# Due times for the last norm's operations, and for the conversions of the down weights in later rounds

## Chip, cores and metric

The kernel runs on one core of a Trainium2 chip. The metric is the time of one launch on the device in microseconds (us), as a median over runs; lower is better. All numbers are float32 at the interface. Matrix products run as three passes over a high and a low part of each operand, so that they keep float32 accuracy.

## The reference

An encoder of two layers on 1024 tokens of width 1024. Each layer mixes tokens (attention in layer 0, a pooling mixer in layer 1), attends to a memory, and applies a gated feed-forward network (FFN). A last RMS norm ends it. What bears on this change is the FFN's second product and that last norm:

```python
def rmsnorm(x, gain):
    y = x * lax.rsqrt(jnp.mean(x * x, axis=-1, keepdims=True) + EPS)
    return y * gain

def conv_gated_ffn(h, w_up, conv_w, conv_b, w_down):     # D_FF = 2816
    u = h @ w_up
    up = jnp.pad(u, ((0, 0), (1, 1), (0, 0)))
    u = up[:, :-2] * conv_w[0] + up[:, 1:-1] * conv_w[1] + up[:, 2:] * conv_w[2] + conv_b
    gate, val = u[..., :D_FF], u[..., D_FF:]
    return (jax.nn.silu(gate) * val) @ w_down

for i in range(2):
    ...                                                  # mixer, cross-attention
    x = x + conv_gated_ffn(rmsnorm(x, ffn_norm[i]), ...)
return rmsnorm(x, final_norm)
```

## The kernel before

**Rows.** The 1024 tokens lie in eight tiles of 128 rows, X0 to X7, each 1024 wide. "Row t" below is such a tile.

**The FFN's second product.** The gated values and `w_down` are multiplied by Strassen-like products: seven block products (numbers 1 to 7 in the table `PRODUCTS`) take the place of eight. The inner dimension is cut into units q of 256. The units are worked off in three rounds (`ROUNDS`, line 48): units 0 to 2, 3 to 6 and 7 to 9 in layer 0, and 0 to 2, 3 to 6 and 7 to 10 in layer 1. Within a round there are two groups g of four rows. Each group goes through the seven products in a fixed order, and each product is one accumulation on PE over the round's units, followed by one addition on DVE that reads the PSUM bank and adds it to half a row of X (line 1699). `plan_phase` (line 1708) writes all this down, and `plan_down` (line 1680) one product.

**Weights.** For each unit q, `plan_W` (line 1653) asks for four loads from HBM into scratch tiles (`scr`, six buffers for the whole kernel, line 658). They bring the operands B21 and B22 (one load), B11, T1 and T2 (one load), T3 and T4 (one load). Each of the seven operands is then converted: ACT copies it to its high part (line 664) and DVE subtracts that to get the low part (line 667), into a half slot of SBUF (40 halves in all). A scratch tile is free again when all its operands are converted. `plan_G` (line 1623) does the same for the gated values. The first product of a group in all but the last one uses B21, then follow B11, T1, T2, B22, T3 and T4.

**The order on the engines.** Nothing is issued in the order of the Python text. The class `Plan` (line 161) collects operations with an engine, a rough cost from the table `KINDS`, what they read and write, and the buffers that they take. PE's operations keep their order, and a clock runs along with PE's work. Every other operation gets a due time: with `late=`, it is PE's clock at that place of the text plus `late`; without it, it is infinite at first. `run` (line 228) then walks backwards and sets each due time to the smallest of (due time of a user of its result minus its own lag). So an operation without `late` is due just in time for PE, when PE uses its result in the end; when nobody does, its due time stays infinite. DVE, ACT, POOL and SP then take work by due time, the earliest first, as soon as inputs and buffers are there, and never more than 30 us of plan time ahead of it (`AHEAD`). An operation that takes a buffer is held back while operations with an earlier due time would lack one. The result is a fixed order of instructions for each engine; on the chip each engine works in that order and waits at each instruction for its inputs.

In these terms, before the change:

- The conversions of a round's units q have due times of 3, 6 or 9 us ahead of the round's first product, the same for all seven operands of a unit, but for the last unit of the round. That one has no `late`, so each operand is due for the product that uses it.
- The last norm's operations (`plan_final`, line 1752, in layer 1 alone) have no `late`, and no product reads their results. Their due time is infinite. For rows 0 to 6 they are: a sum of squares on ACT (line 726), two small POOL operations that make the reciprocal root (lines 718 and 720), one multiplication on DVE by root and gain (line 1747), and one store (line 1750). Row 7 is cut into parts: squares of the upper half and of a first quarter on ACT (line 1768), the gain on the upper half (line 1772, DVE), a sum (line 1776, DVE), the last quarter's squares and their sum (lines 1780 and 1782, DVE), the root (line 1786, POOL), then the upper half's scaling on ACT (line 1790) and the lower half's on DVE (line 1747), and two stores.

In the last round of layer 1 the second group runs its seven products first for rows 4 and 5 and then for rows 6 and 7, so rows 0 to 3 are complete at the end of the first group, and rows 4 and 5 in the middle of the second.

Of the kernel before, what the change touches and what calls it, by code (L numbers as in the profile page):

```python
# [628 lines left out]
class Kernel:  # L629
# [898 lines left out]
    def ffn_main(self, i, U, X, Xd, extra, out, begin):  # L1528
# [5 lines left out]
        C, fixed, half = {}, {}, U.half  # L1534
# [118 lines left out]
        def plan_W(plan, q, late):  # L1653
            def fetch(j):
                raws[q, j] = self.scr()
                if j < 2:
                    w = len(WAT[j]) * 512
                    nc.sync.dma_start(out=raws[q, j][:, :w], in_=wd[(2 * q + 1 - j) * P:(2 * q + 2 - j) * P, :w])
                else:
                    nc.sync.dma_start(out=raws[q, j].rearrange("p (n c) -> p n c", n=2),  # L1660
                                      in_=WT[q][2 * (j - 2):2 * (j - 1)].rearrange("n p c -> p n c"))

            def high(n, j, h):
                x = WD[q, n] = R.get_half()
                self.high(U.halves(x)[0], raws[q, j][:, h * 512:(h + 1) * 512])

            def low(n, j, h):
                self.low(*U.halves(WD[q, n]), raws[q, j][:, h * 512:(h + 1) * 512])
            for j, names in enumerate(WAT):
                raw = ("wraw", q, j)  # L1670
                plan.add("load", len(names) / 2, partial(fetch, j), (), [raw], [("scr", raw)])
                for h, n in enumerate(names):
                    k = ("w", q, n)
                    plan.add("copy", 512, partial(high, n, j, h), [raw], [k], [("half", k)], [raw])
                    plan.add("add", 512, partial(low, n, j, h), [raw, k], [k], uses=[raw, k], late=late)
                    plan.ended[k] = lambda n=n: R.put_half(WD.pop((q, n)))
# [31 lines left out]
        def plan_phase(plan, homes):  # L1708

            home = [X[t] for t in homes]  # L1710

            def plan_back(ts):
                for t in ts:
                    def back(t=t):
                        X[t] = home[t]
                        nc.sync.dma_start(out=X[t], in_=Xd[t * P:(t + 1) * P, :])
                    plan.add("load", 1, back, (), [(f"X{homes[t]}", j) for j in range(2)] + [("row", t, j) for j in range(2)])
            plan_back(range(NT - 2))
            if out is not None:
                plan_gain(plan)  # L1720
            for r, qs in enumerate(rounds):
                for k, q in enumerate(qs):
                    plan_W(plan, q, -3.0 * (len(qs) - 1 - k) if k < len(qs) - 1 else None)
                for g in range(2):
                    end = out is not None and (r, g) == (len(rounds) - 1, 1)
                    order = (1, 2, 6, 5, 7, 3, 4) if end else (2, 1, 5, 6, 3, 7, 4)
                    for js in ((0,), (1,)) if end else ((0, 1),):
                        for n in order:
                            plan_G(plan, r, qs, g, U.PRODUCTS[n][0], js)
                        for n in order:  # L1730
                            for j in js:
                                plan_down(plan, r, qs, g, js, j, n, *[(slice(0, 256), slice(256, 512))] * (end and (j, n) == (1, 4)))
                                yield
                                if (r, g, n, j) == (0, 0, 2, 0):
                                    plan_back(range(NT - 2, NT))


        last = {}

        def plan_gain(plan):  # L1740
            def fetch():
                last["gain"] = self.bcast(self.a["final_norm"])
            plan.add("load", 1, fetch, (), ["gain"], [("scr", "gain")], late=100.0)

        def scaled(t, r, c):
            x = X[t][:, c]
            nc.vector.scalar_tensor_tensor(x, x, r, last["gain"][:, c], op0=OP.mult, op1=OP.mult)

        def leave(t, c):
            nc.sync.dma_start(out=out[t * P:(t + 1) * P, c], in_=X[t][:, c])  # L1750

        def plan_final(plan, t, n, m):

            row, r, lo, hi = [("row", t, h) for h in range(2)], ("fr", t), slice(0, 512), slice(512, 1024)

            def junk(k):
                h = R.get_half()
                plan.ended[k] = lambda: R.put_half(h)
                return R.hv(h)

            def square():
                last[t] = self.row_rstd(X[t], junk(("fjunk", t)))

            def part(k, c):
                if t not in last:
                    last[t] = self.stat(4, "ss4")
                x = X[t][:, c]
                nc.scalar.activation(junk(("fjunk", t, k))[:, c], x, AF.Square, scale=D ** -0.5, accum_out=last[t][:, k:k + 1])

            def gained():  # L1770
                x = X[t][:, hi]
                nc.vector.tensor_tensor(out=x, in0=x, in1=last["gain"][:, hi], op=OP.mult)

            def sums():
                s = last[t]
                nc.vector.tensor_scalar(s[:, 0:1], s[:, 0:1], s[:, 1:2], EPS, op0=OP.add, op1=OP.add)

            def rest():
                s, x = last[t], X[t][:, 256:512]
                nc.vector.scalar_tensor_tensor(junk(("fjunk", t, 2))[:, 256:512], x, 1.0 / D, x, op0=OP.mult, op1=OP.mult,  # L1780
                                               accum_out=s[:, 2:3])
                nc.vector.tensor_tensor(out=s[:, 2:3], in0=s[:, 2:3], in1=s[:, 0:1], op=OP.add)

            def root():
                s = last[t]
                nc.gpsimd.tensor_tensor(out=s[:, 3:4], in0=s[:, 2:3], in1=self.mh[:, :1], op=OP.pow)

            def other():
                x = X[t][:, hi]
                nc.scalar.activation(x, x, AF.Copy, scale=last[t][:, 3:4])  # L1790

            def plan_part(kind, w, f, k, rows, writes):
                j = ("fjunk", t, k)
                plan.add(kind, w, f, rows, writes, [("half", j)], [j])

            if t < NT - 1 and n in (3, 4):
                j = ("fjunk", t)
                plan.add("square", 1024, square, row, [r], [("half", j)], [j])
                plan.add("tap", 1024, lambda: scaled(t, last[t], slice(0, 1024)), [r, "gain", *row], row, uses=["gain"])
                plan.add("load", 1, lambda: leave(t, slice(0, 1024)), row)  # L1800
            elif t == NT - 1 and n == 7:
                plan_part("square", 512, partial(part, 0, hi), 0, row[1:], [(r, 0)])
                plan.add("add", 512, gained, ["gain", *row[1:]], row[1:], uses=["gain"])
            elif t == NT - 1 and not m:
                plan_part("square", 256, partial(part, 1, slice(0, 256)), 1, row[:1], [(r, 1)])
                plan.add("tiny", 1, sums, [(r, 1)], [(r, 0)])
            elif t == NT - 1:
                plan_part("tap", 256, rest, 2, [(r, 0), *row[:1]], [(r, 2)])
                plan.add("scale", 1, root, [(r, 2)], [r])
                plan.add("copy", 512, other, [r, *row[1:]], row[1:])  # L1810
                plan.add("tap", 512, lambda: scaled(t, last[t][:, 3:4], lo), [r, "gain", *row[:1]], row[:1], uses=["gain"])
                for c, k in ((hi, row[1:]), (lo, row[:1])):
                    plan.add("load", 0.5, partial(leave, t, c), k)


        hl, raw = {}, {}
# [287 lines left out]
```

## Time and profile before

| what | value |
|---|---|
| median of 3 runs | 2538.62 us (2538.28 to 2541.3) |
| the profiled execution's own time | 2542.65 us |
| its span in the profile | 2540.9 us |
| granted TensorE clock | 0.996 |
| PE busy | 2486.5 us (98%) |
| DVE busy | 1998.7 us (79%) |
| ACT busy | 1350.8 us (53%) |
| POOL busy | 402.6 us (16%) |

The span is the time from the first to the last instruction in the profile, and it is 1.75 us shorter than the execution's own time. All instants below ("at 2519.24") are microseconds from the start of that span. "SPq" is the queue on which SyncE issues DMAs. A row of the timeline has the start, the busy time, the engine, the line, the operation, its tiles and a count; in brackets stands the idle time just before it and what ended it.

### The profile page before, as it was taken

How to read it: one execution, taken by the hardware profiler on the slowest of the kernel's cores; microseconds unless marked ns; L12 is line 12 of the kernel's file. 1: busy time of each engine (PE TensorE's matmuls, PEld its weight loads, DVE VectorE, ACT ScalarE, POOL GpSimd, SP SyncE). 2: the span in 40 equal slices, each digit the busy share in tenths (PEclk: the TensorE clock that was granted, in tenths of full speed). 3: DMA queues.
4: the chain of work that ended last, by engine and by line, in shares of the span. 5: the costliest groups of instructions: out<-in, count | busy, mean ns of one | idle time of the engine just before them, and what ended most of it. 6: DMA issues, size and time to landing. Idle time of an engine off the chain costs nothing.

```text
span 2540.9 us, 37074 instructions
## 1 busy us (share of the span) xinstructions
PE 2486.5 (98%) x13481; PEld 2132.1 (84%) x13481; DVE 1998.7 (79%) x2946; ACT 1350.8 (53%) x2301; POOL 402.6 (16%) x532
## 2 busy tenths in 40 slices
PE   8999999999999999999999999999999999999996
PEld 8998888888898888888877888889888888887785
DVE  7879999974986389888878766887469888878773
ACT  5558888862555255455455425545346455545441
POOL 5664554530001000000000003002000000000002
PEclk9999999999999999999999999999999999999998
DMA  4300000042595124333358654488124432447661
GB/s 157 94 18 1 2 1 1 1 158 71 172 320 185 62 72 124 93 115 104 94 174 273 205 161 118 138 279 297 60 67 116 117 111 83 118 138 259 221 197 70
DMA packets 306507, 320.71 MB, mean 126 GB/s; under 512 B 12821, under 2 KB 244349, under 8 KB 306325
## 3 DMA queue, kind: packets, MB, share of 16 engines
q1 hardware_dynamic: 306325, 318.35, 39.1%
q8 instruction: 106, 1.74, 0.3%
q14 instruction: 76, 0.62, 0.1%
HBM read 230.90 MB, written 82.58 MB: 123 GB/s over the span
## 4 chain that ended last, share of the span: by engine, by line
PE 82%; DVE 9%; ACT 3%; DMA 3%; issue 3%; POOL 1%; SPq 0%; DVEq 0%; POOLq 0%; ACTq 0%
PE pB L745 21%; PE pB L747 21%; PE pB L746 21%; PE pA L747 3%; PE pA L745 3%; PE pA L746 3%; PE pA L778 2%; DVE nm L788 2%; PE pB L739 2%; DVE R L667 2%; PE pB L1133 1%; DVE PT L673 1%; PE pB L1134 1%; ACT scr L791 1%; ACT R L664 1%
## 5 line engine op out<-in xcount | busy, mean ns | idle before, releaser
L745 PE MATMUL pB<-R,R 128*128 128x512 f32 (+1 forms) x2743 | 1020.5, 372 | 10.3 <-DVE X L1699 2.9
L746 PE MATMUL pB<-R,R 128*128 128x512 f32 (+1 forms) x2743 | 1013.2, 369 | 0.0
L747 PE MATMUL pB<-R,R 128*128 128x512 f32 (+1 forms) x2733 | 1009.8, 369 | 3.3 <-DVE R L667 3.2
L745 PEld LDWEIGHTS pB<-R,R 128*128 128x128 f32 x2743 | 517.6, 189 | 104.2 <-DVE X L1699 3.7
L747 PEld LDWEIGHTS pB<-R,R 128*128 128x128 f32 x2733 | 515.7, 189 | 91.2 <-DVE R L667 5.0
L746 PEld LDWEIGHTS pB<-R,R 128*128 128x128 f32 x2743 | 517.8, 189 | 85.7 <-DVE R L673 0.3
L664 ACT ACTIVATE R<-scr 128x512 fp32r<-128x512 f32 (+2 forms) x340 | 254.3, 780 | 245.5 <-PE pB L746 77.4
L667 DVE TENSOR_TENSOR R<-scr,R 128x512 fp32r<-128x512 f32 (+2 forms) x340 | 289.7, 882 | 30.1 <-ACT R L664 30.0
L718 POOL TENSOR_SCALAR ms<-ss 128x1 f32<-128x1 f32 (+2 forms) x101 | 36.8, 364 | 1702.9 <-ACT R L726 1298.9
L667 DVE TENSOR_TENSOR R<-X,R 128x512 fp32r<-128x512 f32 x374 | 252.2, 685 | 66.5 <-ACT R L664 65.6
L664 ACT ACTIVATE R<-X 128x512 fp32r<-128x512 f32 x374 | 231.8, 630 | 135.2 <-PE pB L746 65.5
L437 ACT COPY scr<-pB 128x512 f32<-128x512 f32 x156 | 91.3, 586 | 194.3 <-PE pB L747 182.6
L1699 DVE TENSOR_TENSOR X<-pB,X 128x512 f32<-128x512 f32 (+1 forms) x145 | 99.2, 686 | 87.2 <-PE pB L747 85.6
L794 POOL TENSOR_SCALAR scr<-scr,inv 128x1024 f32<-128x1024 f32 x125 | 141.0, 1128 | 163.0 <-DVE inv L793 159.4
L673 DVE TENSOR_TENSOR PT<-pB,PT 128x512 fp32r<-128x512 f32 x256 | 163.8, 680 | 1.7 <-ACT PT L672 0.7
L791 ACT ACTIVATE scr<-pA,nm 128x1024 f32<-128x1024 f32 x125 | 139.7, 1117 | 41.3 <-DVE nm L788 40.1
L788 DVE TENSOR_REDUCE nm<-pA 128x1 f32<-128x1024 f32 x125 | 152.4, 1219 | 0.0
L745 PE MATMUL pA<-R,R 128*128 128x512 f32 (+1 forms) x420 | 150.8, 359 | 1.4 <-ACT R L664 1.4
L747 PE MATMUL pA<-R,R 128*128 128x512 f32 (+1 forms) x420 | 150.4, 358 | 0.3 <-DVE R L667 0.3
L746 PE MATMUL pA<-R,R 128*128 128x512 f32 (+1 forms) x420 | 150.0, 357 | 0.2 <-DVE R L667 0.2
L778 PE MATMUL pA<-R,R 128*128 128x512 f32 x512 | 145.0, 405 | 0.0
L672 ACT ACTIVATE PT<-pB 128x512 fp32r<-128x512 f32 x256 | 138.9, 596 | 11.0 <-PE pB L739 9.8
(160 smaller groups left out, 3510.3 us busy)
## 6 DMA issues: line engine op xcount, KB each, us to landing
X<-in_ffn_w_up SPq DMA_DIRECT2D x82, 512.0 KB
Gs<-X SPq DMA_DIRECT2D x105, 256.0 KB
scr<-in_ffn_w_down SPq DMA_DIRECT2D x45, 512.0 KB
scr<-Wt SPq DMA_DIRECT2D x42, 512.0 KB
scr<-Gs SPq DMA_DIRECT2D x35, 512.0 KB
scr<-in_xattn_w_kv SPq DMA_DIRECT2D x32, 512.0 KB
scr<-Gs SPq DMA_DIRECT2D x42, 384.0 KB
scr<-in_attn_w_qkv SPq DMA_DIRECT2D x22, 512.0 KB
```

The lines of the kernel that those rows point to most:

```text
L664: self.nc.scalar.activation(hi, src, AF.Copy)
L667: self.nc.vector.tensor_tensor(out=lo, in0=src, in1=hi.bitcast(F32), op=OP.subtract)
L672: nc.scalar.activation(hi, src, AF.Copy)
L673: nc.vector.tensor_tensor(out=lo, in0=src, in1=hi.bitcast(F32), op=OP.subtract)
L745: mm(out, ah, bh, start=start, stop=False)
L746: mm(out, ah, bl, start=False, stop=False)
L747: mm(out, al, bh, start=False, stop=stop)
L778: nc.tensor.matmul(s[:, kh * 512:(kh + 1) * 512], q, R.v(K[part][kh], 4)[:, kv], start=part == 0, stop=part == 1)
L788: nc.vector.tensor_reduce(nm, s, axis=AX.X, op=OP.max, negate=True)
L791: nc.scalar.activation(pr, s, AF.Exp, bias=nm, accum_out=rs)
L794: nc.gpsimd.tensor_scalar(pr, pr, ri, 1.0, op0=OP.mult, op1=OP.mult)
L1699: nc.vector.tensor_tensor(out=x, in0=banks[b][:, c], in1=x, op=OP.add)
```

## The change

In `plan_phase`, the early due times of the weights' conversions stay for round 0 alone. In rounds 1 and 2 of both layers all units now have none of their own, so each operand is due for the product that uses it. In `plan_final`, every operation of the last norm gets a `late` of 2.5 to 8 us after the product that completes its row (or half, or quarter).

```diff
-                    plan_W(plan, q, -3.0 * (len(qs) - 1 - k) if k < len(qs) - 1 else None)
+                    plan_W(plan, q, -3.0 * (len(qs) - 1 - k) if k < len(qs) - 1 and not r else None)
...
             def plan_part(kind, w, f, k, rows, writes):
                 j = ("fjunk", t, k)
-                plan.add(kind, w, f, rows, writes, [("half", j)], [j])
+                plan.add(kind, w, f, rows, writes, [("half", j)], [j], late=2.5)
 
             if t < NT - 1 and n in (3, 4):
                 j = ("fjunk", t)
-                plan.add("square", 1024, square, row, [r], [("half", j)], [j])
-                plan.add("tap", 1024, lambda: scaled(t, last[t], slice(0, 1024)), [r, "gain", *row], row, uses=["gain"])
-                plan.add("load", 1, lambda: leave(t, slice(0, 1024)), row)
+                plan.add("square", 1024, square, row, [r], [("half", j)], [j], late=3.0)
+                plan.add("tap", 1024, lambda: scaled(t, last[t], slice(0, 1024)), [r, "gain", *row], row, uses=["gain"], late=6.0)
+                plan.add("load", 1, lambda: leave(t, slice(0, 1024)), row, late=8.0)
             elif t == NT - 1 and n == 7:
                 plan_part("square", 512, partial(part, 0, hi), 0, row[1:], [(r, 0)])
-                plan.add("add", 512, gained, ["gain", *row[1:]], row[1:], uses=["gain"])
+                plan.add("add", 512, gained, ["gain", *row[1:]], row[1:], uses=["gain"], late=4.0)
             elif t == NT - 1 and not m:
                 plan_part("square", 256, partial(part, 1, slice(0, 256)), 1, row[:1], [(r, 1)])
-                plan.add("tiny", 1, sums, [(r, 1)], [(r, 0)])
+                plan.add("tiny", 1, sums, [(r, 1)], [(r, 0)], late=3.0)
             elif t == NT - 1:
                 plan_part("tap", 256, rest, 2, [(r, 0), *row[:1]], [(r, 2)])
-                plan.add("scale", 1, root, [(r, 2)], [r])
-                plan.add("copy", 512, other, [r, *row[1:]], row[1:])
-                plan.add("tap", 512, lambda: scaled(t, last[t][:, 3:4], lo), [r, "gain", *row[:1]], row[:1], uses=["gain"])
+                plan.add("scale", 1, root, [(r, 2)], [r], late=3.0)
+                plan.add("copy", 512, other, [r, *row[1:]], row[1:], late=4.0)
+                plan.add("tap", 512, lambda: scaled(t, last[t][:, 3:4], lo), [r, "gain", *row[:1]], row[:1], uses=["gain"], late=4.0)
                 for c, k in ((hi, row[1:]), (lo, row[:1])):
-                    plan.add("load", 0.5, partial(leave, t, c), k)
+                    plan.add("load", 0.5, partial(leave, t, c), k, late=6.0)
```

## The prediction, written before the result was known

> **What bounds the kernel now.** I read the page first: engines, slices, chain.
>
> ```profile
> PE 2486.5 (98%) x13481; PEld 2132.1 (84%) x13481; DVE 1998.7 (79%) x2946; ACT 1350.8 (53%) x2301; POOL 402.6 (16%) x532
> PE   8999999999999999999999999999999999999996
> PE 82%; DVE 9%; ACT 3%; DMA 3%; issue 3%; POOL 1%; SPq 0%; DVEq 0%; POOLq 0%; ACTq 0%
> ```
>
> PE is busy for 98% of the span, so 54.4 us of 2540.9 are left. Only two things can shorten the run: less PE waiting, or a shorter stretch after PE's last product. The last slice of the PE row is a 6 and not a 9, so part of those 54 us lies at the end. Next I cut the second FFN into stages (round 1, the two groups of the last round, the rest after them); columns are length, then busy time of PE, PEld, DVE, ACT and POOL with counts, PE clock, DMA share and GB/s.
>
> ```profile
> 2364.30:2442.50 78.20, 78.14 (x344) 64.67 (x345) 58.79 (x80) 35.05 (x49) 0.00 (x0) 1.00 0.67 218
> 2442.50:2481.00 38.50, 38.50 (x171) 31.90 (x170) 21.89 (x31) 12.00 (x18) 0.00 (x0) 1.00 0.47 144
> 2481.00:2519.30 38.30, 38.21 (x180) 31.92 (x179) 12.14 (x19) 1.26 (x2) 0.00 (x0) 1.00 0.00 0
> 2519.30:2540.90 21.60, 0.00 (x0) 0.00 (x0) 11.59 (x15) 9.12 (x19) 13.49 (x15) 0.61 0.48 194
> ```
>
> The last row is the target: 21.6 us without one PE instruction. In the stage ahead of it DVE is busy for 12.14 of 38.3 us, ACT for 1.26, POOL for nothing. So the work of the last stage has room where PE still runs. What fills the last stage is in the timeline, by engine.
>
> ```profile
> 2513.65 0.69 DVE L1699 TENSOR_TENSOR X<-pB,X 128x512 f32<-128x512 f32 x1 [2.03 <-PE pB L747]
> 2516.37 0.69 DVE L1699 TENSOR_TENSOR X<-pB,X 128x512 f32<-128x512 f32 x1 [2.03 <-PE pB L747]
> 2519.24 0.75 DVE L1699 TENSOR_TENSOR X<-pB,X 128x256 f32<-128x256 f32 x2 [2.18 <-PE pB L747]
> 2522.26 1.28 DVE L1747 SCALAR_TENSOR_TENSOR X<-X,rs,scr 128x1024 f32<-128x1024 f32 x1 [2.26 <-POOL rs L720]
> 2524.26 1.28 DVE L1747 SCALAR_TENSOR_TENSOR X<-X,rs,scr 128x1024 f32<-128x1024 f32 x1 [0.72 <-POOL rs L720]
> 2533.47 0.68 DVE L1772 TENSOR_TENSOR X<-X,scr 128x512 f32<-128x512 f32 x1
> 2534.08 0.21 DVE L1776 TENSOR_SCALAR ss<-ss 128x1 f32<-128x1 f32 x1
> 2534.66 0.16 DVE L1782 TENSOR_TENSOR ss<-ss 128x1 f32<-128x1 f32 x1
> 2534.74 1.28 DVE L1747 SCALAR_TENSOR_TENSOR X<-X,rs,scr 128x1024 f32<-128x1024 f32 x1
> 2536.47 0.75 DVE L1747 SCALAR_TENSOR_TENSOR X<-X,ss,scr 128x512 f32<-128x512 f32 x1 [0.44 <-POOL ss L1786]
> 2519.76 0.42 ACT L1768 ACTIVATE R<-X 128x256 fp32r<-128x256 f32 x1 [32.90 <-DVE X L1699]
> 2520.08 0.19 ACT L1768 ACTIVATION_READ_ACCUMULATOR R<-X 128x1 f32 x1
> 2520.18 1.04 ACT L726 ACTIVATE R<-X 128x1024 fp32r<-128x1024 f32 x1
> 2521.12 0.19 ACT L726 ACTIVATION_READ_ACCUMULATOR R<-X 128x1 f32 x1
> 2521.39 0.19 POOL L718 TENSOR_SCALAR ms<-ss 128x1 f32<-128x1 f32 x1 [635.45 <-ACT R L726]
> 2521.67 0.55 POOL L720 TENSOR_TENSOR rs<-ms,mh 128x1 f32<-128x1 f32 x1
> 2524.31 1.29 POOL L718 TENSOR_SCALAR ms<-ss 128x1 f32<-128x1 f32 x1
> 2534.90 1.53 POOL L1786 TENSOR_TENSOR ss<-ss,mh 128x1 f32<-128x1 f32 x1 [0.33 <-DVE ss L1782]
> 2523.57 14.48 SPq L1750 DMA_DIRECT2D out<-X  x9
> ```
>
> All seven whole rows are normed here, after the last addition, one every 2.0 us (multiplications at 2522.26, 2524.26 and so on), and row 7's own short chain (from L1776 at 2534.08) comes after six of them. The pace is POOL's: 1.29 + 0.55 us a row. The first addition of row 7's last half ends at 2519.67, its squares on ACT at 2520.27 (2520.08 + 0.19), yet L1776, which only adds those two sums, starts at 2534.08. That wait is the queue's order, nothing else.
>
> The other place is the start of layer 1's round 1, in the waits of PE, the timeline and the chain of waits (the last four rows, which have no engine's idle time).
>
> ```profile
> PE pB L745 <- DVE X L1699: 2.6, 1, 2.6
> PE pB L747 <- DVE R L667: 1.3, 1, 1.3
> 2364.36 0.50 PE L745 MATMUL pB<-R,R 128*128 128x512 f32 x1 [2.58 <-DVE X L1699]
> 1394.37 0.50 PE L745 MATMUL pB<-R,R 128*128 128x512 f32 x1 [0.31 <-DVE X L1699]
> 2360.61 3.10 DVE L667 TENSOR_TENSOR R<-scr,R 128x512 fp32r<-128x512 f32 x5 [0.95 <-ACT R L664]
> 2363.62 0.68 DVE L1699 TENSOR_TENSOR X<-pB,X 128x512 f32<-128x512 f32 x1
> DMA packets 6623, 10.87 MB, mean 311 GB/s; under 512 B 385, under 2 KB 3804, under 8 KB 6620
> 2353.35 5.44 DMA scr<-Wt
> 2358.90 1.69 ACT R L664 x3
> 2360.61 1.16 DVE R L667 x2
> 2361.82 1.30 DVE R L667 x3
> ```
>
> PE stands for 2.58 us because an addition stands behind five weight conversions on DVE, whose last load took 5.44 us to come. The packets' row is that of the 35 us ahead of the stall: the DMA engines moved 311 GB/s, so a burst of weights is late there. The like place of layer 0 shows 0.31 us. The 1.3 us belong to round 0, whose due times stay.
>
> **Part 1: the last norm between the additions.** One accumulation takes 2.72 us in the last round (additions at 2513.65 and 2516.37). Rows 0 to 5 are complete seven of them, 19 us, ahead of PE's end. Each needs on ACT 1.04 + 0.19 = 1.23 us, on POOL 0.19 to 1.29 plus 0.55, on DVE 1.28 and one store of 0.5 MB. DVE gets 6 x 1.28 + 0.68 (L1772) = 8.4 us in a stretch where it idles 16.6 + 26.2 us. Additions are due 1.5 us after their product and multiplications 6 us, so an addition goes first. The wait that is added on DVE is a multiplication waiting for POOL. Behind it stand additions, and behind those PE. From the end of a row's squares to its multiplication it took 2522.26 - 2521.31 = 0.95 us, so the block can be about that long, where the next product gives 2.03 us of idle time before each addition. I cost it at zero; without that cover it would be 6 x 0.95 = 5.7 us. The stores pass SPq while the last group's loads are issued; the stage from 2481 on moves 0 GB/s, so they collide with nothing late.
>
> Row 6 is completed by the addition at 2516.37 (ends 2517.06). Squares to 2518.3, root at 2519.2, so its multiplication is ready at about 2519.3, as row 7's last additions run. By the due times row 7's sum (late 3.0) goes before row 6's multiplication (late 6.0).
>
> Row 7: squares end at 2520.27, a handoff from ACT takes 0.08 (POOL at 2521.39 after 2521.31), so L1776 starts at 2520.35. In the trace of before it is 2540.9 - 2534.08 = 6.82 us from that instruction to the end: sums, root, scaling, and the last stores, with one whole row's multiplication at 2534.74 right behind the sums. In the new order row 6's multiplication would stand exactly there, so I take the same 6.82 us: end at 2527.17, 13.7 us earlier.
>
> One price in that chain has two rows: a POOL step takes 0.19 alone and 1.29 while L1747 runs on DVE; row 7's root took 1.53 beside such a multiplication, against 0.55 for L720 alone. If row 6's multiplication stays clear of the root, 1.53 - 0.55 = 1.0 us more is gained; if it gets ahead of the sums, they wait for up to 1.28 us. So part 1 is worth 12.4 to 14.7 us, and I take 13.7, the case whose order the trace has. [...]
>
> **Part 2: conversions due product by product.** The same loads, copies and subtractions, in another order; nothing is added. At a round's start four operands of B21 have to be there, not all of the early units' operands. Gain: at most the stalls it can reach, 2.58 + 0.31 = 2.9 us. Against it: the load that brings B21 also brings B22, four products later, so up to four scratch tiles of six (one of which holds the final gain in layer 1) may stand until B22 is converted, and the other loads have to run through the two left. The trace has no such row; the nearest ones give one tile's cycle: 5.44 (DMA) + 1.69 (ACT) + about 1.2 (DVE) = 8.3 us at this load. Cost per boundary: from 0 to the largest stall of this kind, 2.6 us; four boundaries (two in each layer), so 0 to 10.4. I take a gain of 1.0, because DMA demand ahead of the boundary falls, the one cause that the trace shows, and expect some waits to come back later in the round.
>
> **Sum.** 13.7 + 1.0 = 14.7 us. The profiled execution took 2542.65, which is 1.75 more than its span of 2540.9; it would become about 2528. The median of the runs shown is 2538.62, which is 4.03 below the profiled execution, so I take the difference off that: 2538.62 - 14.7 = 2523.9, say 2524.
>
> **Rivals.**
> A. *Scratch tiles held too long; slower.* In rounds 1 and 2 four half-used tiles leave two for a product's five loads (four weights, one of gated values). Five loads at 8.3 us on two tiles take 20.8 us, against 5.44 us for the two accumulations of a product over four units (2 x 2.72). Without a lead PE would wait up to 15 us at each of four boundaries. It eats the gain at 13.7 / 4 = 3.4 us each, and is slower beyond 0.2% at 4.7 us each; at 7 us each the time is 2538.6 - 13.7 + 28 = 2553. For it: DMA at 311 GB/s ahead of round 1. Against: loads may run up to 30 us ahead, more than 20.8, and PE lost only 0.06 and 0.00 us of round 1 and the last round's first group. 6%.
> B. *New waits, net loss in part 2.* As A, but 1 to 2.6 us a boundary, or DVE full in the last round's first group: there it idles 16.6 us; if all 21 subtractions of three units (0.62 each, 3.10 / 5) moved in, and four rows' multiplications, 13.0 + 5.1 = 18.1 would not fit. With 4 to 10.4 us lost and the gain of 1.0 not had, 2529 to 2535. 17%.
> C. *The norm stays at the end in part.* Its squares need a half slot of SBUF, and free slots are few in the last round; if three rows stayed behind they cost 2.0 us each: 2524 + 6 = 2530. Against: slots come free with each product. 5%.
> D. *Nothing changes:* due times only sort; if the order came out as before, 2538.6. The infinite due times explain the tail too well. 2%.
>
> **How the numbers follow.** Forecast 70% (2520 to 2528: ends 14.7 + 2.9 = 17.6 off, and 12.4 with 2 us lost). A 6%, B 17%, C 5%, D 2%. The range 2519 to 2531 takes the forecast, C and half of B: about 83%. A difference of 0.2% (5 us) is about what can be told from none. Faster by more than that (under 2533.5): forecast, C and 15 of B's 17, 90%; within: the rest of B, D and 1 of A, 5%; slower: 5%.
>
> **What would show it.** In the profile after: PE's end at 2516 to 2521; rows L726, L718, L720 and six of the L1747 between additions of the last round; between PE's end and the span's end 7 to 8.5 us, not 21.6; L1776 within 1 us of its squares; the 2.58 us stall gone or under 1. I am wrong if PE's waits in rounds 1 and 2 of either layer add up to more than 5 us, above all on L664 or L667 behind a DMA into scr, or if whole rows' multiplications still stand after PE's end other than row 6's.

## The result and the profile after

The changed kernel takes 2522.69 us (2521.86 to 2523.95, six runs), the kernel before 2538.95 us (2538.28 to 2541.3, six runs). The ratio is 0.9935, its 95% interval 0.9922 to 0.9947: 16.3 us less. The forecast was 2524.0. The ratios in this document leave out one slow launch, of the kernel with part 2 alone (2758.75 us, at a granted clock of 0.849). The profiled execution of the changed kernel took 2522.73 us, its span is 2521.0.

Three lines of the changed kernel's page, its engines, its PE slices and its chain:

```profile
PE 2483.8 (99%) x13481; PEld 2130.5 (85%) x13481; DVE 1999.2 (79%) x2946; ACT 1352.0 (54%) x2301; POOL 395.5 (16%) x532
PE   8999999999999999999999999999999999999998
PE 84%; DVE 7%; issue 4%; ACT 2%; DMA 2%; POOL 1%; DVEq 0%; POOLq 0%; SPq 0%; ACTq 0%
```

The engines run as many instructions as before. PE is idle for 37 us of the span, where it was 54. The last slice has gone from 6 to 8. The same four stages as before, now by their new instants (length, busy time of PE, PEld, DVE, ACT and POOL, PE clock, DMA share, GB/s):

```profile
2358.50:2436.40 77.90, 77.90 (x345) 64.52 (x344) 54.67 (x75) 32.12 (x45) 0.00 (x0) 1.00 0.60 203
2436.40:2475.00 38.60, 38.60 (x172) 31.95 (x171) 30.45 (x45) 20.74 (x33) 2.49 (x6) 1.00 0.73 235
2475.00:2513.20 38.20, 38.12 (x180) 31.87 (x178) 18.12 (x25) 7.64 (x14) 3.35 (x9) 1.00 0.16 63
2513.20:2521.00 7.80, 0.00 (x0) 0.00 (x0) 3.37 (x8) 1.23 (x3) 1.52 (x1) 0.73 0.34 134
```

The stage without PE is 7.8 us long and was 21.6. Its work has moved to the two stages ahead of it: DVE has gone from 21.89 to 30.45 us and from 12.14 to 18.12, POOL from nothing to 2.49 and 3.35, and PE is as full there as it was. The timeline of the changed kernel's end, first DVE, then ACT, then POOL:

```profile
2496.69 0.69 DVE L1699 TENSOR_TENSOR X<-pB,X 128x512 f32<-128x512 f32 x1 [0.84 <-PE pB L747]
2497.29 1.27 DVE L1747 SCALAR_TENSOR_TENSOR X<-X,rs,scr 128x1024 f32<-128x1024 f32 x1
2499.41 0.69 DVE L1699 TENSOR_TENSOR X<-pA,X 128x512 f32<-128x512 f32 x1 [0.84 <-PE pA L747]
...
2513.16 0.76 DVE L1699 TENSOR_TENSOR X<-pB,X 128x256 f32<-128x256 f32 x2 [2.18 <-PE pB L747]
2514.16 0.21 DVE L1776 TENSOR_SCALAR ss<-ss 128x1 f32<-128x1 f32 x1 [0.25 <-ACT R L1768]
...
2514.82 1.28 DVE L1747 SCALAR_TENSOR_TENSOR X<-X,rs,scr 128x1024 f32<-128x1024 f32 x1
2516.54 0.75 DVE L1747 SCALAR_TENSOR_TENSOR X<-X,ss,scr 128x512 f32<-128x512 f32 x1 [0.44 <-POOL ss L1786]
2513.94 0.19 ACT L1768 ACTIVATION_READ_ACCUMULATOR R<-X 128x1 f32 x1
2512.61 0.55 POOL L720 TENSOR_TENSOR rs<-ms,mh 128x1 f32<-128x1 f32 x1
2514.98 1.52 POOL L1786 TENSOR_TENSOR ss<-ss,mh 128x1 f32<-128x1 f32 x1 [1.83 <-DVE ss L1782]
```

A whole row's multiplication (2497.29, 1.27 us long) sits between two additions, and each addition still waits for PE alone. Only one whole row, row 6 at 2514.82, is left behind the last addition. L1776 follows its squares (2513.94 + 0.19 = 2514.13) by 0.03 us, where it stood 13.8 us behind them. From the last addition at 2513.16 to the end it is 7.84 us; before it was 2540.9 - 2519.24 = 21.66.

PE's waits in the changed kernel, from 2280 to the end (engine, line, waited for: us in total, times, longest):

```profile
PE pB L747 <- DVE R L667: 1.0, 1, 1.0
PE pB L745 <- DVE scr L439: 0.3, 1, 0.3
```

The stall of 2.6 us on the addition (L1699) is gone, and both waits that are left belong to round 0.

**Where the span's 19.9 us come from.** The tail gave 21.66 - 7.84 = 13.82. The last addition starts 2519.24 - 2513.16 = 6.08 us earlier, so PE came to its end 6.08 us earlier. I followed this by setting the same PE instruction of both kernels side by side. The difference was already 1.28 us at 1311.71, ahead of the first instruction whose order the change touches. It grew by 0.6 us at the start of layer 0's round 1, by 1.3 in layer 1's mixer, and by 2.9 at the start of layer 1's round 1, and not after that. A second profile of the changed kernel (the last run below) gives the same 0.6 and 2.9 at these two starts. The mixer's 1.3 us are no work of the change. Windows of before, then of after, over the same work:

```profile
1592.20:1595.50 3.30, 3.30 (x18) 3.30 (x17) 0.80 (x2) 0.00 (x0) 0.00 (x0) 0.50 0.02 5
```

```profile
1590.50:1593.80 3.30, 3.30 (x30) 3.30 (x29) 2.22 (x3) 0.73 (x1) 0.00 (x0) 1.00 0.02 5
```

In the profiled execution of before PE's granted clock was 0.50 for 3.3 us, and 18 matmuls ran where 30 do. So part 2 is worth 0.6 + 2.9 = 3.5 us in this pair of profiles, and 1.28 + 1.3 = 2.6 us belong to the two executions that were profiled. What is left, 19.9 - 2.6 = 17.3 us, agrees with the medians: they differ by 16.3 us, and by the interval of the ratio it is 13.5 to 19.8.

### The profile page after: what moved, and what is told of

Read it like the earlier page. It is cut to its first block, busy times and chain, and to the rows that moved or that the text cites. A ratio compares the mean times of both kernels' runs of the same rounds, so it can differ in the third digit from the quotient of the medians.

```text
span 2521.0 us, 37054 instructions
## 1 busy us (share of the span) xinstructions
PE 2483.8 (99%) x13481; PEld 2130.5 (85%) x13481; DVE 1999.2 (79%) x2946; ACT 1352.0 (54%) x2301; POOL 395.5 (16%) x532
## 4 chain that ended last, share of the span: by engine, by line
PE 84%; DVE 7%; issue 4%; ACT 2%; DMA 2%; POOL 1%; DVEq 0%; POOLq 0%; SPq 0%; ACTq 0%
PE pB L745 22%; PE pB L747 22%; PE pB L746 21%; PE pA L747 3%; PE pA L745 3%; PE pA L746 3%; PE pA L778 2%; DVE nm L788 2%; PE pB L739 2%; PE pB L1133 1%; DVE PT L673 1%; PE pB L1134 1%; DVE R L667 1%; ACT scr L791 1%; PE pB L323 1%
## 5 line engine op out<-in xcount | busy, mean ns | idle before, releaser
L664 ACT ACTIVATE R<-scr 128x512 fp32r<-128x512 f32 (+2 forms) x340 | 255.4, 781 | 230.1 <-DMA scr<-Gs 66.8
L667 DVE TENSOR_TENSOR R<-scr,R 128x512 fp32r<-128x512 f32 (+2 forms) x340 | 290.4, 882 | 21.7 <-ACT R L664 21.3
L667 DVE TENSOR_TENSOR R<-X,R 128x512 fp32r<-128x512 f32 x374 | 252.1, 685 | 66.0 <-ACT R L664 65.2
L664 ACT ACTIVATE R<-X 128x512 fp32r<-128x512 f32 x374 | 231.6, 630 | 134.9 <-PE pB L746 67.8
L718 POOL TENSOR_SCALAR ms<-ss 128x1 f32<-128x1 f32 (+2 forms) x101 | 30.5, 302 | 1688.9 <-ACT R L726 1284.8
L437 ACT COPY scr<-pB 128x512 f32<-128x512 f32 x156 | 91.3, 586 | 196.0 <-PE pB L747 190.3
L1699 DVE TENSOR_TENSOR X<-pB,X 128x512 f32<-128x512 f32 (+1 forms) x145 | 99.3, 687 | 85.0 <-PE pB L747 82.8
```

The source lines that it names most:

```text
L664: self.nc.scalar.activation(hi, src, AF.Copy)
L667: self.nc.vector.tensor_tensor(out=lo, in0=src, in1=hi.bitcast(F32), op=OP.subtract)
L1699: nc.vector.tensor_tensor(out=x, in0=banks[b][:, c], in1=x, op=OP.add)
```

## The experiments

Kernels that were timed together ran beside the kernel before on one chip. Its median there was 2540.37 us for the first four below, 2541.24 for round 0 earlier, row 6 last, the additions ahead in the sorting and B22 by itself, and 2541.57 for the two with slower loads in the plan and the changed kernel again. Each difference below is against the one beside it.

**Part 1 alone.** The line for the conversions' due times is that of before, the last norm's due times are the new ones.

```diff
-                    plan_W(plan, q, -3.0 * (len(qs) - 1 - k) if k < len(qs) - 1 and not r else None)
+                    plan_W(plan, q, -3.0 * (len(qs) - 1 - k) if k < len(qs) - 1 else None)
```

> The changed kernel with the old due times of the weights' conversions in all rounds: part 1 alone. My theory (the tail is worth 13.8 us by itself, part 2 the 2.6 us stall and 0.3 us): the stretch after PE's last product is 7.8 us as in the changed kernel, the wait of about 2.6 us for an addition at the start of layer 1's round 1 is back, and the median is 2525.2 (2524 to 2526.5). Rival (part 2 is worth the whole 6 us by which PE ends earlier in the two profiles): PE ends 6 us later than in the changed kernel, median 2528.7.

Measured: 2526.4 us (2524.5 to 2527.29), ratio 0.9945 (0.9931 to 0.9958), 14.0 us less. From its last addition to the end it is 2525.5 - 2517.69 = 7.8 us, as in the changed kernel. PE's waits from 2280 on:

```profile
PE pB L745 <- DVE X L1699: 1.8, 1, 1.8
PE pB L747 <- DVE R L667: 1.0, 1, 1.0
PE pB L745 <- DVE scr L439: 0.3, 1, 0.3
```

The wait on the addition is back, 1.8 us this time. The tail's 13.7 us of the prediction are the gain of this kernel. The reading in which all 6.08 us of PE's earlier end belong to part 2 would have made it 2528.7, which is 10.2 us less than the 2538.95 of the first comparison, and it falls.

**Part 2 alone.** The last norm without due times, the conversions as changed: every `late=` that the change added to `plan_final` is taken out.

```diff
-                plan.add("tap", 1024, lambda: scaled(t, last[t], slice(0, 1024)), [r, "gain", *row], row, uses=["gain"], late=6.0)
+                plan.add("tap", 1024, lambda: scaled(t, last[t], slice(0, 1024)), [r, "gain", *row], row, uses=["gain"])
```

> The kernel before with the new due times of the weights' conversions alone: part 2 alone. My theory: the tail after PE's last product stays at 21.7 us, no wait of PE at the start of layer 1's round 1, PE ends about 3 us earlier; median 2536 (2535 to 2537). Rival (part 2 is worth 6 us): 2532.9. Second rival (tiles held too long; part 2 alone costs time and the norm hid it): over 2539.

Measured: 2537.38 us, ratio 0.999 (0.9981 to 0.9999), 3.0 us less; by the interval it is 0.3 to 4.8. PE's waits from 2270 on:

```profile
PE pB L747 <- DVE R L667: 1.0, 1, 1.0
PE pB L745 <- DVE X L1699: 0.4, 1, 0.4
```

The 1.0 us belong to round 0; the 0.4 us, at 2360.98, are an addition in the last product ahead of round 1. 14.0 + 3.0 = 17.0 us, and together the two parts give 16.3. So they add up within what the intervals allow.

**Additions first.** What lets the stall go: that conversions no longer stand ahead of the addition on DVE, or that less has to be loaded and converted ahead of the round? Part 1 alone, and the additions due 12 us ahead of their product's end instead of 1.5 us behind it.

```diff
-                plan.add("add", w, partial(read, c), [k, ("row", t, h)], [("row", t, h)], uses=[b], late=1.5)
+                plan.add("add", w, partial(read, c), [k, ("row", t, h)], [("row", t, h)], uses=[b], late=-12.0)
```

> As part 1 alone, with the old early conversions, but the additions that read PE's banks are due 12 us before their product instead of 1.5 us after it, so DVE's order puts them ahead of any conversion that is due then. Theory 1 (the 2.6 us stall is the order on DVE: an addition queued behind conversions that wait for a late load): the stall is under 0.5 us although the loads come as early and as thickly as before; median as the changed kernel, 2522.7 (2521.5 to 2524). Theory 2 (the stall is the amount of data asked for at once): PE waits 2 to 3 us for conversions at the first products of round 1 instead; median 2525.

Measured: 2559.94 us (2557.53 to 2560.37), ratio 1.0077 (1.0063 to 1.0091), 19.6 us more. PE's waits around layer 1's FFN, from 2270 on:

```profile
PE pB L745 <- ACT scr L437: 13.1, 1, 13.1
PE pB L747 <- DVE R L667: 2.8, 1, 2.8
```

A miss: neither theory had this. A due time travels backwards through everything that an operation needs, so the operands of the whole second product became due 12 us earlier too. Layer 1 shows it in a wait of 13.1 us for the up-projection's last values (L437), and in layer 0 the like wait is 20.6 us. The kernel says nothing on the question that it was made for.

**Round 0 product by product too.** The rule that the change keeps for round 0 is dropped.

```diff
-                    plan_W(plan, q, -3.0 * (len(qs) - 1 - k) if k < len(qs) - 1 and not r else None)
+                    plan_W(plan, q, None)
```

> The changed kernel with the early due times gone from round 0 as well, which the change left alone. Theory 1 (early due times only crowd DVE and the loads): the waits of 1.0 us and 0.3 us in layer 1's round 0 and of about 2.3 us in layer 0's shrink, median 2520 to 2522. Theory 2 (round 0 has no earlier round's buffers to wait for and needs its weights early, because the up-projection still fills DVE and the loads): new waits of PE there, median 2524 to 2530.

Measured: 2532.13 us (2527.75 to 2533.47), ratio 0.9966 (0.9954 to 0.9979): 8.2 us less than before, so 8 us of the gain are lost. PE's waits in layer 1 from 2270 on:

```profile
PE pB L746 <- DVE R L667: 2.3, 1, 2.3
PE pB L747 <- DVE R L667: 1.9, 1, 1.9
PE pB L745 <- DVE X L1699: 1.6, 1, 1.6
```

PE waits for low parts of weights (L667) and for an addition. A weight that comes just in time by the plan comes late on the chip here. Set beside the kernel before at the same PE instructions, this one lost 4.8 us in layer 1's round 0 and 3.3 us in layer 0's. Layer 0's loss goes with the clock: behind two waits of 1.6 and 1.8 us the granted clock was 0.50 from 1346.95 to 1353.80.

**Round 0 earlier.** The other direction: all units of round 0 due 6 us ahead of it.

```diff
-                    plan_W(plan, q, -3.0 * (len(qs) - 1 - k) if k < len(qs) - 1 and not r else None)
+                    plan_W(plan, q, None if r else -6.0)
```

> The changed kernel with a due time of 6 us ahead for all units of round 0, the last one too, which was due product by product. Theory 1 (round 0 needs its weights early, and its waits of 1.0 us in layer 1 and of about 2.3 us in layer 0 come from late operands): 1 to 2.5 us less, median 2520 to 2522. Theory 2 (those waits are DVE's own load from the up-projection's last values, and weights due earlier only push it back): 2523 to 2530.

Measured: 2532.17 us (2530.69 to 2535.4), ratio 0.9966 (0.9954 to 0.9978), 9.1 us less than before, so 7 us of the gain are lost. PE's one wait from 2280 on, and the window right behind it:

```profile
PE pB L745 <- DVE scr L439: 5.5, 1, 5.5
2298.50:2304.70 6.20, 6.20 (x15) 4.85 (x16) 4.41 (x5) 2.77 (x5) 0.00 (x0) 0.50 0.35 115
```

The old waits are gone and a single one of 5.5 us has come, for the end of the up-projection (L439), which the earlier conversions push back; layer 0 has the same 5.5. The wait is not all that it costs: behind it PE ran for 6.2 us at a granted clock of 0.50, with 15 matmuls where the next 3.4 us hold 16, and in layer 0 for 4.9 us (1327.00 to 1331.90). If half the clock is half the work, that is (6.2 + 4.9) / 2 = 5.6 us more, as an estimate; against it stand the shorter waits that are gone. The steps of 3 us that round 0 keeps lie between two slopes.

**Row 6 last.** Row 6's multiplication and store are planned behind row 7's, so that row 7's root has DVE to itself. One execution.

```diff
                 plan.add("square", 1024, square, row, [r], [("half", j)], [j], late=3.0)
+                if t == NT - 2:
+                    return
...
+                u, whole, other_row = t - 1, slice(0, 1024), [("row", t - 1, h) for h in range(2)]
+                plan.add("tap", 1024, lambda: scaled(u, last[u], whole), [("fr", u), "gain", *other_row, *row[:1]], other_row, uses=["gain"], late=8.0)
+                plan.add("load", 1, lambda: leave(u, whole), other_row, late=10.0)
```

> The changed kernel with row 6's multiplication and its store moved behind row 7's lower half, so that no whole-row multiplication runs on DVE while POOL makes row 7's root. If the root is slow because of that multiplication beside it: the root takes 0.55 us instead of 1.52, row 7's scaling starts 1.0 us earlier, and row 6's store now ends last, so the stretch after PE's end stays at 7.5 to 8.1 us. Rival (the root's 1.52 us is its own price, whatever runs beside it): the root takes 1.5 us again and the stretch grows to about 9 us.

Measured: 2524.89 us, with a span of 2523.1. The timeline's end:

```profile
2515.08 0.76 DVE L1699 TENSOR_TENSOR X<-pB,X 128x256 f32<-128x256 f32 x2 [2.18 <-PE pB L747]
...
2517.49 0.75 DVE L1747 SCALAR_TENSOR_TENSOR X<-X,ss,scr 128x512 f32<-128x512 f32 x1 [0.66 <-POOL ss L1786]
2518.16 1.27 DVE L1747 SCALAR_TENSOR_TENSOR X<-X,rs,scr 128x1024 f32<-128x1024 f32 x1
2516.91 0.55 POOL L1786 TENSOR_TENSOR ss<-ss,mh 128x1 f32<-128x1 f32 x1 [1.82 <-DVE ss L1782]
```

The root takes 0.55 us and not 1.52, so the neighbour on DVE was the cause. The tail has nevertheless not become shorter: 2523.1 - 2515.08 = 8.0 us, against 7.84. Row 6's multiplication now ends last, at 2519.43, and 3.7 us later its store is the end; in the changed kernel row 7's lower half ended last, at 2517.29, and it too was 3.7 us to the end. What one row gains the other pays.

**Additions ahead in the sorting alone.** The question that the third kernel left: part 1 alone, with the additions of rounds 1 and 2 sorted 12 us earlier after the due times have travelled, so that their operands keep theirs.

```diff
+        for op in self.ops:
+            op["due"] -= op.get("ahead", 0.0)
...
+                plan.ops[-1]["ahead"] = 12.0 if r else 0.0
```

> As part 1 alone, with the old early conversions, but in rounds 1 and 2 the additions that read PE's banks are sorted 12 us earlier, without making anything that they depend on due earlier. Theory 1 (the stall at layer 1's round 1 is the order on DVE: an addition queued behind conversions that wait for a late load): no wait of PE over 0.5 us there, median as the changed kernel, 2523 (2522 to 2524.5). Theory 2 (the early loads ask for too much data at once, and the order matters little): PE waits 1.5 to 3 us there, for a conversion or an addition, median 2525 to 2526.

Measured: 2527.51 us (2526.27 to 2529.81), ratio 0.9948 (0.9935 to 0.9962), the same as part 1 alone. PE's longest wait from 2280 on, and DVE's rows around it in the timeline (line numbers are two higher in this kernel):

```profile
PE pB L747 <- DVE X L1701: 2.6, 1, 2.6
```

```profile
2361.64 3.10 DVE L669 TENSOR_TENSOR R<-scr,R 128x512 fp32r<-128x512 f32 x5 [0.97 <-ACT R L666]
2364.66 0.68 DVE L1701 TENSOR_TENSOR X<-pB,X 128x512 f32<-128x512 f32 x1
```

The five conversions still stand ahead of the addition, although it has the earlier due time by far. So sorting is not what put them there. What did is read from the plan's text and not measured: it takes whatever is ready by its own clock. By that clock the conversions' loads were there before the product's end, on the chip they were not, and the addition, which could have run, stands behind them.

**Slower loads in the plan.** If that is so, a plan that knows of longer loads should order it right. Part 1 alone, with weights' loads of rounds 1 and 2 planned 3 us longer.

```diff
                 plan.add("load", len(names) / 2, partial(fetch, j), (), [raw], [("scr", raw)])
+                plan.ops[-1]["lag"] += slow
...
+                    plan_W(plan, q, -3.0 * (len(qs) - 1 - k) if k < len(qs) - 1 else None, 3.0 if r else 0.0)
```

> As part 1 alone, with the old early conversions, but the planner is told that the weights' loads of rounds 1 and 2 take 3 us longer (6.5 us plus the conversion instead of 3.9 for half a megabyte), so it places their conversions later in DVE's fixed order. Theory 1 (the stall is a fixed order made with a load time that is too short, 3.9 us planned against 5.4 measured): the addition comes ahead of the five conversions, the wait of 2.6 us at the start of layer 1's round 1 is under 0.5 us, and the time is that of the changed kernel within 1 us. Theory 2 (the early due times ask for more data than the DMA engines and the scratch tiles can bring by then, whatever order DVE has): PE waits 1.5 us or more around there and the time is 2 to 4 us over the changed kernel.

Measured: 2528.27 us (2527.58 to 2529.91), ratio 0.9951 (0.9936 to 0.9965), 13.3 less than before; part 1 alone had 14.0. PE's waits from 2280 on, then the window of the 3.3 us behind the first of them:

```profile
PE pB L745 <- ACT R L664: 1.7, 1, 1.7
PE pB L747 <- DVE R L667: 1.4, 2, 1.1
```

```profile
2360.60:2363.90 3.30, 3.30 (x9) 2.57 (x10) 2.27 (x4) 0.96 (x2) 0.00 (x0) 0.53 1.00 309
```

The addition no longer stalls PE, and another wait of 1.7 us has come in its place, for a high part (L664) whose load was late. Behind it PE ran at a granted clock of 0.53 for 3.3 us, with the DMA engines full (1.00, 309 GB/s). So an order that fits the loads better doesn't remove the wait. What is left as the cause is that much is asked for at once ahead of the round. Part 2 asks for less there: in the 35 us ahead of layer 1's round 1 SPq issued 11 loads of weights in the kernel before and 8 in the changed one (10.82 MB and 9.99 MB moved in all). Whether the loads count or the conversions that hang on them, no run here separates.

**The changed kernel with slower loads in the plan.** All loads of weights and of gated values planned 1.5 us longer.

```diff
             plan.add("load", w / 1024, fetch, [("G", q, n) for q in qs], [raw], [("scr", raw)])
+            plan.ops[-1]["lag"] += 1.5
...
                 plan.add("load", len(names) / 2, partial(fetch, j), (), [raw], [("scr", raw)])
+                plan.ops[-1]["lag"] += 1.5
```

> The changed kernel with the planner told that all loads of weights and gated values of the second product take 1.5 us longer, which is what the trace shows ahead of layer 1's round 1. Theory 1 (the waits left in round 0, about 2.3 us in layer 0 and 1.3 us in layer 1, are conversions placed too early for their loads): 1 to 3 us less than the changed kernel. Theory 2 (round 0 is bound by DVE and the up-projection's last values): within 1 us of it or up to 5 us over it, because loads are also due earlier.

Measured: 2526.76 us (2525.79 to 2528.07), ratio 0.9944 (0.9929 to 0.9959), 2.75 us more than the changed kernel beside it. PE's waits in layer 1:

```profile
PE pB L747 <- DVE R L667: 2.0, 2, 1.5
PE pB L745 <- ACT scr L437: 1.4, 1, 1.4
```

The up-projection's last values (L437) come later, and in layer 0 that wait is 4.2 us. It fits that loads which start earlier take room ahead of round 0, but nothing here shows that by itself. Longer loads in the plan gained nothing.

**B22 by itself.** Rival A of the prediction: four half-used scratch tiles hold up later loads. B22 gets a load of its own, so that B21's tile is free as soon as B21 is converted.

```diff
-        WAT = (("B21", "B22"), ("B11",), ("T1", "T2"), ("T3", "T4"))
+        WAT = (("B21",), ("B11",), ("T1", "T2"), ("T3", "T4"), ("B22",))
```

> The changed kernel with B22 loaded by itself, when its own product needs it, so that no scratch tile waits four products long half used; one more load per unit in all rounds. If the held tiles are why the DMA engines stand nearly idle for 5 us just ahead of layer 1's round 1 (share 0.14): that hole closes (share over 0.5). My theory of the time: PE does not wait there either way, so the median is 2522.7, within 1.5 us. Rival (held tiles cost time elsewhere in rounds 1 and 2): 2520 or less.

Measured: 2524.0 us (2523.39 to 2525.05), ratio 0.9934 (0.992 to 0.9947), which is the changed kernel's. Windows ahead of layer 1's round 1, of the changed kernel first and then of this one:

```profile
2340.00:2345.00 5.00, 5.00 (x24) 4.14 (x23) 4.35 (x7) 2.50 (x4) 0.00 (x0) 1.00 0.91 334
2345.00:2350.00 5.00, 5.00 (x24) 4.14 (x23) 4.64 (x8) 3.67 (x6) 0.00 (x0) 1.00 0.14 45
```

```profile
2340.00:2345.00 5.00, 5.00 (x23) 4.13 (x22) 4.04 (x6) 3.77 (x6) 0.00 (x0) 1.00 0.65 215
2345.00:2350.00 5.00, 5.00 (x24) 4.13 (x22) 4.49 (x8) 2.08 (x3) 0.00 (x0) 1.00 0.71 228
```

In the changed kernel the DMA engines fall from a share of 0.91 to 0.14 for 5 us. With B22 apart the hole closes to 0.71, as it would if held tiles were its cause. That cause isn't shown beyond doubt: the order of the loads changed too, and from 2324 to 2375 SPq still waits for scratch tiles that a conversion holds, 31.5 us in total against 30.8. PE is full in both, and the time is the same: DVE, busy for 4.64 of those 5 us, had work in hand.

**The changed kernel again**, beside the two with slower loads.

> The changed kernel itself beside the two others on the same chip: 0.9935 of the kernel before, as measured at first. If it is not within 0.1% of that, the comparisons of single kernels with it across chips are worth less.

Measured: 2524.01 us (2523.43 to 2524.14), ratio 0.9933 (0.9916 to 0.995), which is the 0.9935 of the first comparison within 0.1%.

## Why the prediction was right, and where it was off

**Part 1, predicted 13.7.** Right in place and size: 14.0 by itself, 13.82 in the tails of the profiles. The order came out as written: row 7's sums, then row 6's multiplication, then row 7's lower half. From L1776 to the end it is 2521.0 - 2514.16 = 6.84 us, and 6.82 was taken from the trace of before. The root stood beside the multiplication as forecast, and took 1.52 where 1.53 had been read.

**"I cost it at zero"**, the multiplications among the additions. It holds: in the rows above the additions at 2496.69 and 2499.41 wait for PE, each after 0.84 us of idle DVE, and PE has no wait in the last round.

**DVE beside POOL.** In the prediction's rows it is POOL that is slower beside DVE (1.29 us where it takes 0.19 alone). The trace of before also has a row in which DVE is the slower, in the pooling mixer, where POOL works on whole rows:

```profile
1540.69 3.94 DVE L667 TENSOR_TENSOR R<-scr,R 128x512 fp32r<-128x512 f32 x5
1541.10 1.79 POOL L1978 TENSOR_SCALAR scr<-scr,rs 128x1024 f32<-128x1024 f32 x1
```

Five such conversions took 3.10 us at 2360.61, with POOL idle; here they took 0.84 us more. For the norm's POOL steps of 128x1 that price did not come. A timeline of the changed kernel, POOL's step and the conversion beside it, with a conversion that has no such neighbour last:

```profile
2466.07 0.51 POOL L718 TENSOR_SCALAR ms<-ss 128x1 f32<-128x1 f32 x1 [1.95 <-ACT R L726]
2465.85 0.68 DVE L667 TENSOR_TENSOR R<-scr,R 128x512 fp32r<-128x512 f32 x1
2468.57 0.68 DVE L667 TENSOR_TENSOR R<-scr,R 128x512 fp32r<-128x512 f32 x1
```

The conversion, which started first, takes 0.68 us either way; it is POOL's step that takes 0.51 and not 0.19. In the one place of the last round that is like it, at 2476.95, it is the same. Where a root of 128x1 starts first, at 1647.16, the conversion that starts 0.03 us behind it takes 0.71. So the price fell on POOL, where nobody waits for it.

**Part 2, predicted 1.0 of at most 2.9.** This is the term that was mis-sized: 3.0 alone, 16.3 - 14.0 = 2.3 on top of part 1, and 3.5 at the same PE instructions. The medians alone don't show it, as the 0.3 to 4.8 of part 2 alone hold the 1.0 too; the two profiles of the changed kernel do, with the same 0.6 and 2.9 us. The 1.0 was a choice between a gain of 2.9 and a loss of 10.4, not a sum, so that the total came within 1.3 us rests on part 1. The step that failed is "expect some waits to come back later in the round". None did, and the whole of the 2.58 us stall and of layer 0's 0.31 went. The upper bound, the sum of the two stalls, was too low as well: at the same instructions the step at layer 1's round 1 is 2.9 us for a stall of 2.58, and 0.6 for layer 0's 0.31. In the trace of before matmuls overlap: each takes 0.39 us and one starts every 0.23 us. Over the stall it is 2364.36 - 2361.39 = 2.97 us from one start to the next, 2.74 more than 0.23, and the matmuls right behind it come more slowly too (the first took 0.50 us, in the row that the prediction quotes).

**The signs.** All held but one: PE's end was to lie at 2516 to 2521 and lies at 2513.2. The working took off the 4.03 us between the profiled execution and the median at the end of the sum, but not from the instants of the profile. The 1.28 and 1.3 us above, outside the stages that the change reaches, would account for 2.6 of those 4.03 us; no second profile of before is there to show it. One sum of the ranges is off too: 2538.6 - 17.6 is 2521.0, where the forecast's stretch begins at 2520. The 2522.69 lies inside either way.

**Rivals.** A was a correct reading of the buffers with no price: SPq does wait for scratch tiles and the DMA engines do fall idle, and the kernel without the hole takes the same time. It overlooked that what the loads feed, DVE, was the fuller of the two. B did not come: DVE takes 30.45 of 38.6 us in the last round's first group, and PE is busy for all of it. For C, six of seven whole rows left the tail. D is excluded by the order on DVE.

## What to carry to other kernels

Where a queue's order is planned, an operation that nobody waits for drifts to the very end of every queue, and so does the short chain that does set the end and is sorted behind it; give each a due time tied to when its inputs are complete. An early due time for a whole block of loads is a request for all of them at once: in later rounds the due time of the use served better, while the first round, behind busy engines, lost 7 to 8 us in either direction. A wait of PE can cost more than its length: behind the 5.5 us of round 0 earlier PE worked at half clock for another 6.2. Before a gain is read from two profiles, set the same instruction of the busiest engine side by side along the run, so that a difference that began ahead of the change is not booked to it.

## What the hardware showed that was not expected

PE's granted clock halved with no wait of PE over 0.6 us ahead of it. Windows of the kernel before: the two ahead of the half clock that is shown above, and the one behind the 2.58 us stall at layer 1's round 1.

```profile
1585.20:1588.70 3.50, 3.50 (x33) 3.50 (x32) 3.50 (x5) 2.64 (x7) 2.16 (x3) 1.00 0.52 211
1588.70:1592.20 3.50, 3.50 (x30) 3.37 (x29) 2.10 (x3) 2.92 (x6) 0.74 (x2) 1.00 0.20 80
2364.30:2367.60 3.30, 3.24 (x14) 2.67 (x15) 3.18 (x6) 2.14 (x4) 0.00 (x0) 1.00 0.92 306
```

PE is full for 7.0 us, then at 0.50 for 3.3; the longest wait from 1560 to 1600 is 0.6 us. Full means that some matmul ran: 3.8 of the 7.0 us, from 1587.16, went to 32 matmuls of the pooling mixer (L1992), half of them 128x112 and half only 24x16. Whether that matters for the clock no run here shows. Around that place the profile of the additions sorted ahead shows the half clock too (0.50 in one window of 3.3 us), and so does that of part 1 alone (0.63 and 0.85 in two neighbouring windows of 3.3 us); the other ten profiles don't. Behind the stall of 2.58 us the clock is 1.00, while in the kernel with slower loads it was 0.53 behind a stall of 1.7. Elsewhere a slower PE did follow its waits, all in round 0: behind the 20.6 and 13.1 us of additions first a matmul started every 0.43 us and not every 0.23, for 4.0 and 5.3 us; behind the two of 5.5 us in round 0 earlier the clock was 0.50 for 4.9 and 6.2 us; and it was 0.50 also behind 2.1 us in the profile of part 2 alone (1349.65 to 1353.05) and 2.0 us in that of row 6 last (1347.30 to 1350.70). What sets it off stays open.
